# Down projection of a ConvFFN: one level of Strassen's product for the prompt, in one sweep over the weights

## The chip, the cores and the metric

The kernel runs on one core of a Trainium2 chip. Its engines are named as the profile names them: PE (matrix products; PEld is its weight load), DVE, ACT and POOL (elementwise work), and SP, which here only issues transfers (DMA). Each engine works through its own list of instructions in order. The metric is the time of one execution in microseconds.

## The reference, cut to what matters

One layer of a streaming encoder is computed for a prompt of 1024 tokens and for 8 sample streams of 16 new tokens, together 1152 tokens, in fp32. The part that is changed is the end of the layer:

```python
D_MODEL = 1024;  D_FF = 2816;  CONV_W = 3
def conv_ffn(x, prev, w_up, conv_w, conv_b, w_down):
    up = x @ w_up                                     # D_MODEL -> 2*D_FF
    up_p = jnp.concatenate([prev, up], axis=1)        # prev: zeros for the prompt
    c = sum(up_p[:, j:j + L] * conv_w[j] for j in range(CONV_W)) + conv_b
    gate, val = jnp.split(c, 2, axis=-1)
    return (jax.nn.silu(gate) * val) @ w_down, up_p[:, -(CONV_W - 1):]

f, new_conv = conv_ffn(rmsnorm(x, norm2), conv_prev, w_up, conv_w, conv_b, w_down)
x = x + f
...
y = rmsnorm(x, final_g)
```

## The kernel before, in words

Tokens stand in nine tiles of 128: eight of the prompt (`NPT`) and one with all samples. Of `w_down` (2816 x 1024) there are 22 blocks of 128 rows (`NF`, index k), each in two column halves of 512 (`dh`).

All products are of fp32 precision made from three products of rounded numbers: an operand x is split into a high part (written by ACT, type fp32r) and a low part, x minus the high part (written by DVE, by the helper `tt`, whose line in the profile is L86). `mm3` then issues three matmuls, high by high (L61), high by low (L62) and low by high (L63).

The up projection runs over 22 blocks j (gate and value columns) and already uses one level of Strassen's product: for each j `prep` makes seven weight operands `op` (sums on POOL, splits on ACT and DVE), `product` multiplies, `collect` adds the seven products into `ext`, and `up_pair_end` does the convolution, the silu and the product `g`, and stores g of block j (features by tokens) to DRAM in `g_d`. Such a block takes 22.2 us. The last store of g, j = 21, falls into the beginning of the down projection.

The down projection works in two groups of tokens, tiles 0 to 4 and then tiles 5 to 8. For each it runs over both column halves and for each of these over all k. `down_k` loads a weight tile 128x512 (`wd`, five buffers) and splits it (`wdh` by ACT on L1489, `wdl` by DVE); it also splits the activations (`gh`, L1503, and `gl`) which `reload` has brought back from `g_d` as `gr` (L1452). So each weight is loaded and split twice, 88 tiles in all, and there are 9 x 2 x 22 x 3 = 1188 matmuls of 128x512. The sums stand in PSUM, one bank for each tile (`acc`). For the last five k (`TAILK`) of the last half, the loop goes tile by tile, so that the closing normalization of one tile runs beside the matmuls of the next. The residual rows X (`x3`, 128x1024 each) and the vector `fgb` are loaded at k = 14, and `conv_out` writes the convolution state; an order is imposed there by hand:

```python
if dh == 0 and k == 14:
    with tc.issue_after(WD[COUNT[0] - 1].ins):
        ...
        load_x3()
```

Otherwise the order of instructions on each engine, SP's loads among them, is not the one in which the code is written. A scheduler of the framework (`schedule_with_timeline_sim=True`) orders each engine's list from the data dependences, the buffers and its own estimate of times. All loads and stores are issued on SP, which works them off in that order; an issue that has to wait holds up those behind it. In the listings of order, `waits DMAHW5_49` is such a wait for one of eight DMA completion counters, used in turn, and `waits DVE_49` a wait for DVE.

Of the kernel before, what the change touches and what calls it, by code (L numbers as in the profile page):

```python
# [13 lines left out]
OP = mybir.AluOpType  # L14
# [31 lines left out]
def emit(ctx, tc, x_prompt, x_sample, cache_k, cache_v, state_ssm_re, state_ssm_im, state_conv,  # L46
# [21 lines left out]
    def pool(name, bufs=1, **kw):  # L68
        return tc.tile_pool(name=name, bufs=bufs, reuse_waits="tile", **kw)
# [1216 lines left out]
    def prep(n):  # L1286

        j, i = divmod(n, 7)
        if j >= NF:
            return  # L1290
        a, b = RAW[j, 0], RAW[j, 1]
        if i == 0:
            s1 = upW.tile([P, 4, P], F32, name=f"S1_{j}", tag="S1", bufs=1)
            gsub(s1, b[:, 0], b[:, 1], OP.add)
            SUMS[j] = dict(A11=a[:, 0], A12=a[:, 1], A22=b[:, 1], S1=s1, S2=a[:, 0], S3=b[:, 0], S4=a[:, 1])
        src = SUMS[j][PROD[i][0]]
        pl = opL if i < 3 else opR
        op = pl.tile([P, 2, 4, P], F32R, name=f"op{n}", tag="op", bufs=3 if i < 3 else 4)
        act(op[:, 0], src, AF.Copy)  # L1299
# [93 lines left out]
    def up_pair_end(j):  # L1393
        cg = upw.tile([P, GLEN], F32, name=f"cg{j}", tag="cg", bufs=1)
        up_conv(j, 0, cg)
        act(cg, cg, AF.Silu)  # L1396
        g = upw.tile([P, GLEN], F32, name=f"g{j}", tag="gs")
        up_conv(j, 1, g)
        tt(g, g, cg, OP.mult)
        nc.sync.dma_start(g_d[j], g)  # L1400

    sts = ExitStack()
    stp = sts.enter_context(pool("stp", side="right"))
    up_begin(0)
# [31 lines left out]
    fu.close()  # L1436
    exs.close()
# [1 line left out]
    h2s.close()  # L1439


    gr0 = ctx.enter_context(pool("gr0"))
    dwA = ctx.enter_context(pool("dwA"))
    gr = ctx.enter_context(pool("gr", side="right"))

    HC = (slice(0, 640), slice(640, GLEN))

    def reload(half, j):
        if j < NF:
            n = HC[half].stop - HC[half].start  # L1450
            GT[half, j] = (gr0 if half == 0 and j < 4 else gr).tile([P, n], F32, name=f"gr{half}_{j}")
            nc.sync.dma_start(GT[half, j], g_d[j, :, HC[half]])  # L1452

    for j in range(4):
        reload(0, j)
    dw = ctx.enter_context(pool("dw", 2, side="right"))
    fgb = dw.tile([P, DM], F32, name="fgb", bufs=1)
    S3 = dw.tile([P, NT, 2], F32, name="S3", bufs=1)

    def conv_out():  # L1460
        cf = cvt.rearrange("p r a -> p (r a)")
        n = NROW * NF2
        outp = [(conv_prompt[0, 0].rearrange("j (a p) -> (j a) p", p=P), 0, 2 * NF2),
                (conv_sample[0].rearrange("b j (a p) -> (b j a) p", p=P), 2 * NF2, n - 2 * NF2)]
        for dst, c0, m_ in outp:
            for i in range(0, m_, P):
                m = min(P, m_ - i)
                pt = pup.tile([P, P], F32, name=f"cvo{c0}_{i}", tag="up")
                nc.tensor.transpose(pt[:m], cf[:, c0 + i:c0 + i + m], ident)  # L1469
                r = dw.tile([P, P], F32, name=f"cvr{c0}_{i}", tag="rows")  # L1470
                V_.tensor_copy(r[:m], pt[:m])
                nc.sync.dma_start(dst[i:i + m], r[:m])

    COUNT, WD = [0], {}

    def down_k(half, dh, k, nt, pl, b):
        dc = slice(dh * 512, dh * 512 + 512)
        nm = f"{half}{dh}{k}"
        w = COUNT[0]
        COUNT[0] += 1  # L1480
        main = pl is dwA

        def op_(x, n):
            return pl.tile([P, n], F32R, name=x + nm, tag=f"{x}{w % 2}" if main else x, bufs=1 if main else b)

        raw = dwA.tile([P, 512], F32, name="wd" + nm, tag=f"wd{w % WDB}")
        WD[w] = nc.sync.dma_start(raw, w_down[0, k * P:(k + 1) * P, dc])
        wh_, wl_ = op_("wdh", 512), op_("wdl", 512)
        act(wh_, raw, AF.Copy)  # L1489
        tt(wl_, raw, f(wh_), OP.subtract)  # L1490
        w5 = 5 * P if main else nt * P
        gh_, gl_ = op_("gh", w5), op_("gl", w5)

        if half == 0:
            segs = [(gh_[:, 0:640], gl_[:, 0:640], GT[0, k])]
        else:
            def smp(x):
                return x[:, 384:512].rearrange("p (b s) -> p b s", s=NS)
            g_ = GT[1, k]
            segs = [(gh_[:, 0:384], gl_[:, 0:384], g_[:, 0:384]),  # L1500
                    (smp(gh_), smp(gl_), g_[:, 384:].rearrange("p (b s) -> p b s", s=NS + 2)[:, :, 2:])]
        for oh_, ol_, src in segs:
            act(oh_, src, AF.Copy)  # L1503
            tt(ol_, src, f(oh_), OP.subtract)
        return gh_, gl_, wh_, wl_

    for half in range(2):
        t0, nt = ((0, 5), (5, 4))[half]
        X3 = {}

        def load_x3():
            for t in range(t0, t0 + nt):
                X3[t] = dw.tile([P, DM], F32, name=f"x3_{t}", tag="x3", bufs=6)
                nc.sync.dma_start(X3[t], x2_d[t * P:(t + 1) * P])

        for dh in range(2):
            dc = slice(dh * 512, dh * 512 + 512)
            last = half == 1 and dh == 1
            acc = {t: pup.tile([P, 512], F32, name=f"acc{t}{dh}", tag="up") for t in range(t0, t0 + nt)}
            ke = NF - TAILK if last else NF  # L1520
            for k in range(ke):
                if half == 0:
                    reload(dh, 4 * (1 - dh) + k)
                gh_, gl_, wh_, wl_ = down_k(half, dh, k, nt, dwA, 2)
                for t in range(t0, t0 + nt):
                    c = slice((t - t0) * P, (t - t0 + 1) * P)
                    mm3(acc[t], gh_[:, c], gl_[:, c], wh_, wl_, k == 0, k == NF - 1)
                if dh == 0 and k == 14:
                    with tc.issue_after(WD[COUNT[0] - 1].ins):
                        if half == 0:  # L1530
                            conv_out()
                            nc.sync.dma_start(fgb, bcast_row(final_g, DM))
                        load_x3()
            ops = [down_k(half, dh, k, nt, *((dwA, 2) if k < ke + 2 else (dw, TAILK - 2))) for k in range(ke, NF)]
            for t in range(t0, t0 + nt):
                for k in range(ke, NF):
                    gh_, gl_, wh_, wl_ = ops[k - ke]
                    c = slice((t - t0) * P, (t - t0 + 1) * P)
                    mm3(acc[t], gh_[:, c], gl_[:, c], wh_, wl_, k == 0, k == NF - 1)
# [44 lines left out]
```

## Time and profile before

| | |
|---|---|
| three runs | 1244.7, 1247.71, 1249.7 us; median 1247.71 |
| the profiled execution | 1247.31 us; span in the profile 1245.2 us |
| mean granted TensorE clock | 0.983 |
| busy, share of the span | PE 95%, PEld 84%, DVE 70%, ACT 52%, POOL 19% |
| moved by DMA | 149.05 MB, 120 GB/s in the mean |
| last matmul of the up projection ends | 954.6 us |
| down projection, matmuls | 956.6 to 1232.2 us |
| end of the last store | 1245.2 us |

Each row of the profile that follows names line, engine, operation, tile written and tiles read, with buffer numbers left out. Shares are means over stages with different bounds, so the rows of a single stage are what counts. "Idle before" is the time in which an engine had nothing to do before an instruction, with what ended it.

### The profile page before, as it was taken

What the parts mean: (1) busy time and instruction counts of PE and PEld (TensorE: products, weight loads), DVE (VectorE), ACT (ScalarE), POOL (GpSimd) and SP (SyncE); (2) the same over time, 40 slices, a digit from 0 to 9 for tenths busy, and PEclk for the clock granted to TensorE, in tenths of its full rate; (3) what the DMA queues carried; (4) which work ended last, traced back from release to release, by engine and by line L of the source; (5) the groups of instructions that cost most, each with busy time, mean ns of one, the idle gap of its engine ahead of it and who ended that gap; (6) DMA issues with size and microseconds to landing.
All of it is one profiled execution on the core that took longest, in us unless ns stands there. A gap on an engine that the chain in (4) does not pass through costs nothing. (4 is left out here: it accounts for less than half of the span.)

```text
span 1245.2 us, 20642 instructions
## 1 busy us (share of the span) xinstructions
PE 1186.4 (95%) x7528; PEld 1047.4 (84%) x7528; DVE 877.4 (70%) x2062; ACT 648.5 (52%) x1425; POOL 237.1 (19%) x276
## 2 busy tenths in 40 slices
PE   8999999999979878999999999999999999999995
PEld 6777776678768668999999999999998778888884
DVE  6898868898358887667676676767766446468655
ACT  7346557754366676454544545445444344355542
POOL 0000000000000112545354453544531000000000
PEclk9999999999999889999999999999999999999998
DMA  7523246649722521222222212222113982227332
GB/s 251 107 88 117 99 104 192 204 140 256 215 73 85 164 90 35 73 76 66 73 88 74 79 63 73 88 74 81 60 66 111 352 315 77 77 80 250 93 102 77
DMA packets 134023, 149.05 MB, mean 120 GB/s; under 512 B 28794, under 2 KB 94210, under 8 KB 133890
## 3 DMA queue, kind: packets, MB, share of 16 engines
q1 hardware_dynamic: 133922, 147.74, 37.3%
q8 instruction: 59, 0.97, 0.3%
q14 instruction: 42, 0.34, 0.1%
HBM read 107.06 MB, written 41.69 MB: 119 GB/s over the span
## 5 line engine op out<-in xcount | busy, mean ns | idle before, releaser
L86 DVE TENSOR_TENSOR op<-ur,op 128x512 fp32r<-128x512 f32 x132 | 117.6, 893 | 127.5 <-ACT op L1299 124.6
L62 PE MATMUL acc<-wdl,gh 128*128 128x512 f32 x396 | 154.5, 392 | 0.2 <-DVE wdl L86 0.2
L63 PE MATMUL acc<-wdh,gl 128*128 128x512 f32 x396 | 153.4, 391 | 0.0
L86 DVE TENSOR_TENSOR gl<-gr,gh 128x640 fp32r<-128x640 f32 (+2 forms) x132 | 69.7, 555 | 100.4 <-ACT gh L1503 100.0
L1299 ACT ACTIVATE op<-ur 128x512 fp32r<-128x512 f32 x132 | 83.0, 632 | 94.2 <-POOL ur L1253 41.1
L1503 ACT ACTIVATE gh<-gr 128x640 fp32r<-128x640 f32 (+2 forms) x132 | 64.1, 519 | 128.4 <-PE acc L62 121.5
L61 PE MATMUL acc<-wdh,gh 128*128 128x512 f32 x396 | 107.6, 392 | 4.0 <-ACT wdh L1489 3.1
L1253 POOL TENSOR_TENSOR S<-ur 128x512 f32<-128x512 f32 x22 | 51.7, 2352 | 232.0 <-DMA ur<-in_w_up_dram 217.1
L61 PEld LDWEIGHTS acc<-wdh,gh 128*128 128x128 f32 x396 | 74.1, 188 | 20.2 <-ACT wdh L1489 3.9
L62 PEld LDWEIGHTS acc<-wdl,gh 128*128 128x128 f32 x396 | 74.8, 189 | 16.8 <-DVE wdl L86 1.1
L63 PEld LDWEIGHTS acc<-wdh,gl 128*128 128x128 f32 x396 | 74.8, 189 | 15.5
L86 DVE TENSOR_TENSOR wdl<-wd,wdh 128x512 fp32r<-128x512 f32 x88 | 60.5, 687 | 7.8 <-ACT wdh L1489 7.6
L1489 ACT ACTIVATE wdh<-wd 128x512 fp32r<-128x512 f32 x88 | 54.3, 618 | 9.1 <-DMA wd<-in_w_down_dram 5.9
L1388 POOL COPY cvt<-ext 128x16 f32<-128x16 f32 x44 | 35.0, 796 | 94.8 <-ACT ext L1359 94.8
L1387 POOL COPY cvt<-ext 128x2 f32<-128x2 f32 x44 | 19.9, 453 | 143.9 <-DVE ext L86 143.9
L1391 DVE SCALAR_TENSOR_TENSOR cg<-ext,cw,cg 128x1168 f32<-128x1168 f32 x22 | 44.1, 2005 | 0.0
L1253 POOL TENSOR_TENSOR ur<-S,ur 128x512 f32<-128x512 f32 x22 | 38.2, 1737 | 18.2 <-DVE op L86 18.1
L61 PE MATMUL po<-oh,sh 128*128 128x512 f32 x72 | 30.1, 418 | 8.2 <-DVE xs L1213 5.7
L1253 POOL TENSOR_TENSOR ur<-ur,ur 128x512 f32<-128x512 f32 x22 | 35.8, 1627 | 1.7
L1100 POOL MEMSET L<- 128x8 f32 x4 | 0.2, 112 | 179.3 <-PE pkv L62 179.3
L63 PE MATMUL pu<-wh_u,hl 128*128 128x512 f32 x72 | 30.2, 420 | 2.8 <-DVE hl L86 2.8
L526 ACT ACTIVATE e<-sc,nm 128x192 f32<-128x192 f32 (+2 forms) x64 | 25.4, 410 | 14.0 <-DVE nm L523 10.8
(1253 smaller groups left out, 3990.2 us busy)
## 6 DMA issues: line engine op xcount, KB each, us to landing
ur<-in_w_up_dram SPq DMA_DIRECT2D x44, 512.0 KB, 3.9
wd<-in_w_down_dram SPq DMA_DIRECT2D x88, 256.0 KB, 2.9
g_d<-g SPq DMA_DIRECT2D x22, 584.0 KB, 2.9
gr<-g_d SPq DMA_DIRECT2D x22, 320.0 KB, 6.4
gr<-g_d SPq DMA_DIRECT2D x22, 264.0 KB, 5.7
wa<-a_d SPq DMA_DIRECT2D x9, 512.0 KB, 3.6
xa_d<-xo SPq DMA_DIRECT2D x9, 512.0 KB, 6.6
xs<-xa_d SPq DMA_DIRECT2D x9, 512.0 KB, 3.9
```

The costliest lines, as they stand in the source:

```text
L61: mm(out, lh, rh, start=first, stop=False, skip_group_check=True)
L62: mm(out, lh, rl, start=False, stop=False, skip_group_check=True)
L63: return mm(out, ll, rh, start=False, stop=last, skip_group_check=True)
L86: V_.tensor_tensor(o, a, b, op=op)
L526: act(e[:, r], pss[r // 2][:, r % 2], AF.Exp, bias=nm[:, r:r + 1], scale=0.125, accum_out=den[:, r:r + 1])
L1253: nc.gpsimd.tensor_tensor(o, a, b, op=op)
L1299: act(op[:, 0], src, AF.Copy)
L1387: nc.gpsimd.tensor_copy(cvt[:, 0:2, ft], ext[:, SEQ:SEQ + 2])
L1388: nc.gpsimd.tensor_copy(cvt[:, 2:, ft].rearrange("p (b j) -> p b j", j=2), es[:, :, NS:])
L1391: stt(o, ext[:, 0:GLEN], cw[:, 0, ft:ft + 1], o, op0=OP.mult, op1=OP.add)
L1489: act(wh_, raw, AF.Copy)
L1503: act(oh_, src, AF.Copy)
```

## The change

The token tiles of the prompt become two halves (tiles 0 to 3 and 4 to 7), the 22 blocks of features two halves of `NK` = 11, the columns two halves (`LO`, `HI`). So activations and weights are 2 x 2 blocks, A(h, q) and B(q, e), and the prompt's result is formed from seven products in place of eight, of which each has 11 k of four pairs of token tiles. A pair is tile p and tile p + 4.

First, in the up projection: `wd_sums` makes four sums of weight blocks (T1 to T4) and stores them in a new DRAM tensor `t_d`. There are 22 calls, one for each half of each k: two loads of 256 KB, four DVE operations of 128x256, one store of 512 KB, with a single buffer `ws`.

Second, in the down projection: one sweep over k = 0 to 10 with the four weight blocks B11, B12, B21 and B22. B11 is multiplied with the four tiles of A(0, 0) into the four banks a; all four are multiplied with the sample tile, which is not split into products, into two further banks; 24 matmuls for each k. Then come six passes of 11 k of 12 matmuls, with T1, T2, B22, T3, B21 and T4, alternately into the four banks b and the four banks a. Between passes DVE adds (`drain`) a set of banks to the halves of X while the next pass fills the other set. The activation sums `su` are made on DVE during the passes from `gr` tiles, which now stay in SBUF: 44 tiles 128x512, each loaded once. The matmuls number 11 x 24 + 66 x 12 = 1056; weight splits 110; drains 30 (28 for the prompt).

The core of the diff:

```diff
+    def wd_sums(i):
+        k, c = divmod(i, 2)
+        c = slice(c * 256, c * 256 + 256)
+        b = upw.tile([P, 4, 256], F32, name=f"ws{i}", tag="ws", bufs=1)
+        b4 = b.rearrange("p (h e) n -> p h e n", e=2)
+        for h in range(2):
+            r = (h * NK + k) * P
+            nc.sync.dma_start(b4[:, h], w_down[0, r:r + P].rearrange("p (e n) -> p e n", e=2)[:, :, c])
+        tt(b[:, 0], b[:, 1], b[:, 0], OP.subtract)
+        tt(b[:, 1], b[:, 3], b[:, 1], OP.subtract)
+        tt(b[:, 3], b[:, 3], b[:, 0], OP.subtract)
+        tt(b[:, 2], b[:, 2], b[:, 3], OP.subtract)
+        nc.sync.dma_start(t_d[k, :, :, c], b)
...
     for j in range(1, NF):
...
             if i == 2:
                 up_pair_end(j - 1)
+            if i == 4:
+                wd_sums(j)
...
-    for half in range(2):
-        t0, nt = ((0, 5), (5, 4))[half]
...
-        for dh in range(2):
...
-            for k in range(ke):
-                if half == 0:
-                    reload(dh, 4 * (1 - dh) + k)
-                gh_, gl_, wh_, wl_ = down_k(half, dh, k, nt, dwA, 2)
-                for t in range(t0, t0 + nt):
-                    c = slice((t - t0) * P, (t - t0 + 1) * P)
-                    mm3(acc[t], gh_[:, c], gl_[:, c], wh_, wl_, k == 0, k == NF - 1)
...
+    def pairs(x, k, g, w, opens, only=None):
+        for p in range(NP2) if only is None else (only,):
+            c = slice(p * P, (p + 1) * P)
+            mm3(bank(x, p, opens and k == 0), g[0][:, c], g[1][:, c], *w, opens and k == 0, k == NK - 1)
...
+    for k in range(NK):
+        w = {}
+        for blk in ("B11", "B12", "B21", "B22"):
+            w[blk] = w_op(blk, k)
+            if blk == "B11":
+                load_g(0, 0, k + 4)
+                g = g_op(GA[0, 0, k])
+                pairs("a", k, g, w[blk], True)
...
+            q, e = int(blk[1]) - 1, int(blk[2]) - 1
+            mm3(smb[e], *sm[q], *w[blk], k == 0 and q == 0, k == NK - 1 and q == 1)
+        load_gs(k + 2)
+        if k >= 4:
+            load_g(1, 0, k - 4)
+            load_g(1, 1, k - 4)
+        if k == 2:
+            conv_out()
+            nc.sync.dma_start(fgb, bcast_row(final_g, DM))
+        if k == 7:
+            load_x(NPT)
...
+    for k in range(NK):
+        w = w_op("T1", k)
+        if k < 4:
+            load_g(1, 0, k + NK - 4)
+            load_g(1, 1, k + NK - 4)
+        elif k < 8:
+            load_x(k - 4)
+        load_g(0, 1, k)
+        if k + 6 < NK:
+            sum_one(k + 6)
+        g = g_op(SU[k])
+        pairs("b", k, g, w, True)
+        tt(SU[k], SU[k], GA[0, 0, k], OP.subtract)
...
+    for p in range(NP2):
+        drain("a", p, 0, LO)
+
+    for k in range(NK):
+        w = w_op("T2", k)
+        if k < 4:
+            load_x(NP2 + k)
...
```

The order of instructions moves with it at three places.

First, SP at the end of the first sweep. `wd34` is the third weight block of k = 8, `wd36` the first of k = 9, `gr01` the tiles of A(0, 1), `x3` the residual rows. Before, around the X loads at k = 14 of the first column half:

```order
L1487 DMA wd0014_11407<-in_w_down_dram 128x512 [waits DMAHW0_49,DVE_49]
...
L1532 DMA fgb_11020<-in_final_g_dram 128x1024 [waits DMAHW3_49]
L1514 DMA x3_0_11468<-x2_d_70 128x1024 [waits DMAHW4_49]
...
L1514 DMA x3_4_11476<-x2_d_70 128x1024 [waits DMAHW0_49]
L1487 DMA wd0015_11480<-in_w_down_dram 128x512 [waits DMAHW1_49,DVE_49]
L1452 DMA gr1_16_12121<-g_d_5452 128x528 [waits DMAHW2_49]
```

and now:

```order
L1515 DMA wd34_11839<-in_w_down_dram 128x512 [waits DMAHW5_49,DVE_49]
L1481 DMA gr01_4_12169<-g_d_5452 128x512 [waits DMAHW6_49]
L1491 DMA x3_1_12196<-x2_d_70 128x1024 [waits DMAHW7_49]
...
L1481 DMA gr01_10_12327<-g_d_5452 128x512 [waits DMAHW7_49]
L1515 DMA wd35_11848<-in_w_down_dram 128x512 [waits DMAHW0_49,DVE_49]
L1491 DMA x3_4_12356<-x2_d_70 128x1024 [waits DMAHW1_49]
...
L1491 DMA x3_7_12431<-x2_d_70 128x1024 [waits DMAHW4_49]
L1515 DMA wd36_11865<-in_w_down_dram 128x512 [waits DMAHW5_49,DVE_49]
```

The loads of A(0, 1) and of X, which the code has in the passes T1 and T2, stand in SP's list ahead of the weights of k = 9 and 10 of the sweep.

Second, DVE in the up projection, block j = 3; `op25` to `op27` are low parts of weight operands of PE, `ws5` and `ws6` the new sums. Before:

```order
L86 TENSOR_TENSOR op25_6271<-ur31_6090,op25_6271 128x512 [waits DMAHW2_49,PE_49,Activation_49]
L86 TENSOR_TENSOR op26_6301<-ur31_6090,op26_6301 128x512 [waits PE_49,Activation_49]
L86 TENSOR_TENSOR ext20_6092<-pu20c_6212,ext20_6092 128x5x64 [waits PE_49]
...
L86 TENSOR_TENSOR op27_6331<-ur30_6088,op27_6331 128x512 [waits Activation_49]
L1391 SCALAR_TENSOR_TENSOR g2_6450<-ext21_6095,cw_3917,g2_6450 128x1168 [waits DVE_49]
```

and now:

```order
L86 TENSOR_TENSOR op25_6288<-ur31_6107,op25_6288 128x512 [waits DMAHW6_49,PE_49,Activation_49]
L86 TENSOR_TENSOR ws5_7053<-ws5_7053 128x256 [waits DMAHW4_49,DMAHW2_49,DVE_49]
L86 TENSOR_TENSOR ws5_7053<-ws5_7053 128x256 [waits DMAHW5_49,DVE_49]
L86 TENSOR_TENSOR ws5_7053<-ws5_7053 128x256 [waits DVE_49] x2
L86 TENSOR_TENSOR op26_6326<-ur31_6107,op26_6326 128x512 [waits PE_49,Activation_49]
...
L86 TENSOR_TENSOR op27_6356<-ur30_6105,op27_6356 128x512 [waits Activation_49]
L1389 SCALAR_TENSOR_TENSOR g2_6475<-ext21_6112,cw_3917,g2_6475 128x1168 [waits DVE_49]
L86 TENSOR_TENSOR ws6_7307<-ws6_7307 128x256 [waits DMAHW6_49,DMAHW0_49]
```

The four operations of a sum stand between operands of PE, the first of them with a wait for its two loads. The scheduler has put two sums into each of the first eleven or so blocks, where the code has one in each.

Third, DVE where the down projection begins; `g21` is the last product of g, whose store follows. Before:

```order
L1390 SCALAR_TENSOR_TENSOR g21_10985<-ext211_10765,cw_3917,g21_10985 128x1168 [waits DMAHW1_49,Activation_49]
L86 TENSOR_TENSOR wdl000_11032<-wd000_11029,wdh000_11031 128x512 [waits DMAHW7_49,Activation_49]
...
L86 TENSOR_TENSOR gl002_11090<-gr0_2_11013,gh002_11089 128x640 [waits DMAHW4_49,PE_49,Activation_49]
L86 TENSOR_TENSOR wdl002_11086<-wd002_11083,wdh002_11085 128x512 [waits DMAHW1_49,Activation_49]
L86 TENSOR_TENSOR g21_10985<-g21_10985,cg21_10978 128x1168 [waits Activation_49]
```

and now:

```order
L1388 SCALAR_TENSOR_TENSOR cg21_11155<-ext210_10931,cw_3917,cg21_11155 128x1168 [waits Activation_49]
L86 TENSOR_TENSOR sl01_11308<-gs0_1_11205,sh01_11307 128x128 [waits DMAHW3_49,Activation_49]
L86 TENSOR_TENSOR sl11_11312<-gs1_1_11207,sh11_11311 128x128 [waits DMAHW4_49,Activation_49]
L86 TENSOR_TENSOR wl0_11214<-wd0_11211,wh0_11213 128x512 [waits DMAHW5_49,Activation_49]
...
L86 TENSOR_TENSOR wl3_11273<-wd3_11270,wh3_11272 128x512 [waits DMAHW0_49,Activation_49]
L1389 SCALAR_TENSOR_TENSOR cg21_11155<-ext210_10931,cw_3917,cg21_11155 128x1168 [waits DVE_49]
...
L86 TENSOR_TENSOR g21_11162<-g21_11162,cg21_11155 128x1168 [waits Activation_49]
```

The first low weight part now stands behind three of the wide operations of the convolution instead of one, and four weight and four sample parts stand ahead of the last product of g.

More of the change, by code (lines that the diff above doesn't have):

```diff
@@ L1439, in emit @@
     h2s.close()
+    pups.close()
     gr0 = ctx.enter_context(pool("gr0"))
@@ L1444, in emit @@
     gr = ctx.enter_context(pool("gr", side="right"))
[L1446 to L1457, printed above, removed]
@@ L1458, in emit, with load_g @@
-    S3 = dw.tile([P, NT, 2], F32, name="S3", bufs=1)
+    dw = ctx.enter_context(pool("dw", side="right"))
+    pdn = ctx.enter_context(pool("pdn", space=PSUM))
+    NP2 = NPT // 2
+    WDB, TAILK = 5, 5
+    GA, GS, SU, X3 = {}, {}, {}, {}
+    def load_g(h, q, k):
+        if k < NK:
+            pl = gr0 if h == q == 0 and k < 4 else gr
+            GA[h, q, k] = pl.tile([P, 512], F32, name=f"gr{h}{q}_{k}")
+            nc.sync.dma_start(GA[h, q, k], g_d[q * NK + k, :, h * 512:h * 512 + 512])
@@ new lines, in load_gs, with load_x, operand @@
+    def load_gs(k):
+        if k < NK:
+            for q in range(2):
+                GS[q, k] = dwA.tile([P, GLEN - SEQ], F32, name=f"gs{q}_{k}", tag=f"gs{q}", bufs=3)
+                nc.sync.dma_start(GS[q, k], g_d[q * NK + k, :, SEQ:])
+    def load_x(t):
+        X3[t] = gr.tile([P, DM], F32, name=f"x3_{t}")
+        nc.sync.dma_start(X3[t], x2_d[t * P:(t + 1) * P])
+    CW, CG, SPARE = [0], [0], []
+    def operand(src, base, count, bufs, spare):
+        w = count[0]
+        count[0] += 1
+        n = src.shape[-1]
+        if spare:
+            hi, lo = (gr.tile([P, n], F32R, name=f"{base}{x}{w}", tag=SPARE.pop()) for x in "hl")
+        else:
+            hi, lo = (dwA.tile([P, n], F32R, name=f"{base}{x}{w}", tag=f"{base}{x}{w % bufs}") for x in "hl")
+        act(hi, src, AF.Copy)
+        tt(lo, src, f(hi), OP.subtract)
+        return hi, lo
@@ new lines, in w_op, with g_op @@
+    def w_op(blk, k, spare=False):
+        w = CW[0]
+        raw = dwA.tile([P, 512], F32, name=f"wd{w}", tag=f"wd{w % WDB}")
+        if blk[0] == "T":
+            src = t_d[k, :, SUM_AT[blk]]
+        else:
+            r, e = (int(blk[1]) - 1) * NK + k, int(blk[2]) - 1
+            src = w_down[0, r * P:(r + 1) * P, e * 512:e * 512 + 512]
+        nc.sync.dma_start(raw, src)
+        return operand(raw, "w", CW, 4, spare)
+    def g_op(src, spare=False):
+        return operand(src, "g", CG, 2, spare)
@@ new lines, in emit, with bank, drain @@
+    BK2 = {}
+    def bank(x, p, opens):
+        if opens:
+            BK2[x, p] = pdn.tile([P, 512], F32, name=f"dn{x}{p}_{CW[0]}", tag=f"{x}{p}")
+        return BK2[x, p]
+    def drain(x, p, h, dc):
+        o = X3[p + NP2 * h][:, dc]
+        tt(o, o, BK2[x, p], OP.add)
+    def pairs(x, k, g, w, opens, only=None):
+        for p in range(NP2) if only is None else (only,):
+            c = slice(p * P, (p + 1) * P)
+            mm3(bank(x, p, opens and k == 0), g[0][:, c], g[1][:, c], *w, opens and k == 0, k == NK - 1)
@@ new lines, in sum_one @@
+    def sum_one(k):
+        SU[k] = gr.tile([P, 512], F32, name=f"su{k}", tag=f"su{k}")
+        tt(SU[k], GA[1, 0, k], GA[1, 1, k], OP.add)
+    for k in range(NK - 5):
+        sum_one(k)
+    for k in range(NK):
[11 more added lines that the diff above has]
+        tt(SU[k], SU[k], GA[0, 0, k], OP.subtract)
+        if k == 1:
+            for e in range(2):
+                o = X3[NPT][:, (LO, HI)[e]]
+                tt(o, o, smb[e], OP.add)
+            half_one(NPT, LO)
+            half_two((NPT,), LO, HI)
@@ new lines, in emit @@
+    for p in range(NP2):
+        drain("a", p, 0, LO)
+    for k in range(NK):
+        w = w_op("T2", k)
+        if k < 4:
+            load_x(NP2 + k)
+        g = g_op(SU[k])
+        pairs("a", k, g, w, False)
+        tt(SU[k], GA[0, 1, k], SU[k], OP.subtract)
+    for p in range(NP2):
+        drain("b", p, 1, HI)
+    for k in range(NK):
+        w = w_op("B22", k)
+        g = g_op(SU[k])
+        pairs("b", k, g, w, False)
+        tt(GA[1, 0, k], GA[0, 0, k], GA[1, 0, k], OP.subtract)
+        SPARE.append(f"su{k}")
@@ new lines, in emit @@
+    for p in range(NP2):
+        drain("a", p, 0, HI)
+    for k in range(NK):
+        w = w_op("T3", k)
+        g = g_op(GA[1, 0, k])
+        pairs("a", k, g, w, False)
+    for p in range(NP2):
+        drain("b", p, 0, HI)
+        half_one(p, HI)
+    for k in range(NK):
+        w = w_op("B21", k)
+        g = g_op(GA[0, 1, k])
+        pairs("b", k, g, w, True)
+    for p in range(NP2):
+        drain("a", p, 1, HI)
+        half_one(NP2 + p, HI)
+    ops = {}
+    for k in range(NK):
+        late = k >= NK - TAILK
+        w = w_op("T4", k, k == NK - 1)
+        g = g_op(GA[1, 1, k], k >= NK - TAILK + 2)
+        if late:
+            ops[k] = g, w
+        else:
+            pairs("a", k, g, w, False)
+        if k == 2:
+            for p in range(NP2):
+                drain("b", p, 0, LO)
+            half_two(tuple(range(NP2)), HI, LO)
@@ L1556 @@
+    for p in range(NP2):
+        for k, (g, w) in ops.items():
+            pairs("a", k, g, w, False, p)
+        drain("a", p, 1, LO)
+        half_two((NP2 + p,), HI, LO)
 _INS = ['x_prompt', 'x_sample', 'cache_k', 'cache_v', 'state_ssm_re', 'state_ssm_im', 'state_conv',
```

116 lines of the change are left out of this document (49 added, 67 removed).

## The prediction

> **What bounds the kernel now.** I read four views: busy time by stretch, the PE timeline of the down projection, the groups, and the DMA rates. By stretch (start:end, length, busy us of PE, its weight loads, DVE, ACT and POOL, granted clock, DMA share, GB/s):
>
> ```profile
> 500.00:954.60 454.60, 454.60 (x3442) 454.41 (x3440) 315.14 (x424) 223.21 (x446) 213.00 (x240) 1.00 0.23 76
> 954.60:1034.00 79.40, 75.45 (x327) 61.53 (x327) 41.52 (x64) 33.04 (x54) 2.23 (x2) 0.98 0.79 283
> 1034.00:1232.20 198.20, 197.95 (x871) 162.78 (x869) 121.16 (x288) 94.25 (x209) 0.00 (x0) 1.00 0.33 105
> 1232.20:1245.20 13.00, 0.00 (x0) 0.00 (x0) 8.20 (x35) 2.89 (x5) 0.00 (x0) 0.70 0.40 161
> ...
> 955.00:960.00 5.00, 3.42 (x11) 2.77 (x12) 5.00 (x7) 3.29 (x4) 2.23 (x2) 0.74 0.47 143
> 975.00:980.00 5.00, 5.00 (x24) 4.14 (x23) 2.04 (x3) 1.91 (x3) 0.00 (x0) 1.00 1.03 406
> 975.00:1010.00 35.00, 35.00 (x157) 28.95 (x156) 14.67 (x22) 12.30 (x19) 0.00 (x0) 1.00 1.04 388
> 1005.00:1010.00 5.00, 5.00 (x25) 4.09 (x24) 2.59 (x5) 1.17 (x2) 0.00 (x0) 1.00 1.02 414
> 965.84:1011.98 46.14, 44.77 (x199) 36.46 (x197) 18.75 (x29) 16.41 (x27) 0.00 (x0) 1.00 0.99 366
> ```
>
> PE fills the up projection and the down projection (954.6 to 1232.2), at full clock after a cold start. But the first 50 us of the down projection are close to a second bound: from 975 to 1010 the DMA engines are full (share 1.04) at 388 GB/s. The PE timeline (start, length, idle before):
>
> ```profile
> 956.58 1.82 PE L61 MATMUL acc<-wdh,gh 128*128 128x512 f32 x5 [1.96 <-ACT wdh L1489]
> ...
> 959.69 0.63 PE L62 MATMUL acc<-wdl,gh 128*128 128x512 f32 x1
> 960.12 0.63 PE L63 MATMUL acc<-wdh,gl 128*128 128x512 f32 x1
> ...
> 962.06 1.30 PE L61 MATMUL acc<-wdh,gh 128*128 128x512 f32 x5
> ...
> 965.46 1.30 PE L61 MATMUL acc<-wdh,gh 128*128 128x512 f32 x5
> ...
> 1160.45 1.07 PE L61 MATMUL acc<-wdh,gh 128*128 128x512 f32 x4
> ...
> 1163.17 1.07 PE L61 MATMUL acc<-wdh,gh 128*128 128x512 f32 x4
> ...
> 1231.78 0.40 PE L63 MATMUL acc<-wdh,gl 128*128 128x512 f32 x1
> ```
>
> Fifteen matmuls from 962.06 to 965.46 are 3.40 us, twelve from 1160.45 to 1163.17 are 2.72: 0.2267 us each, whatever the tile. At 959.69 the step was 0.43: half clock.
>
> **The matmuls.** Of 1188 matmuls 1056 stay: 11 k of 24 in the first sweep (59.8 us, 5.44 each), then six passes of 11 k of 12 (179.5 us, 2.72 each). The 132 removed are 132 x 0.2267 = 29.9 us, on the path. This is all that the change can win.
>
> **The passes, and what feeds them.** Groups (count, then busy us, mean ns):
>
> ```profile
> L86 DVE TENSOR_TENSOR wdl<-wd,wdh 128x512 fp32r<-128x512 f32 x88 | 60.5, 687 | 7.8 <-ACT wdh L1489 7.6
> L1489 ACT ACTIVATE wdh<-wd 128x512 fp32r<-128x512 f32 x88 | 54.3, 618 | 9.1 <-DMA wd<-in_w_down_dram 5.9 <-PE acc L63 3.2
> L86 DVE TENSOR_TENSOR gl<-gr,gh 128x128 fp32r<-128x128 f32 x44 | 12.5, 284 | 0.0
> L86 DVE TENSOR_TENSOR x<-x,acc 128x512 f32<-128x512 f32 x18 | 11.4, 683 | 3.7 <-PE acc L63 3.7
> ```
>
> All splits and sums are 128x512 like these rows: per k of a pass DVE makes a low weight part (0.687), a low activation part (the same shape) and a sum (0.68), 2.06 of 2.72 us; ACT makes two high parts, 1.24. They hide beside PE. The 28 drains (0.683 each) stand between passes, four at a time while the next pass fills the other banks, 2.7 us; I charge 1 us in all, bounds 0 and 6 x 2.0 = 12 (four drains less the 0.66 us that DVE has free in each of the first k). In the sweep DVE has 4 low weight parts, one of 512 and two of 128 per k, 4.0 of 5.44 us. The 22 extra weight splits over before (110 for 88) lie in there.
>
> **The single DMA queue, first sweep.** This is the term that decides. SP issues in order, and the order of the changed program puts the 33 activation loads of the three quadrants that only the passes read, and all nine X tiles, ahead of the last two k of weights. In before, too, the bulk begins behind the last store of g and wd0015 stands behind it:
>
> ```profile
> 965.84 0.33 SPq L1400 DMA_DIRECT2D g_d<-g  x1
> ...
> 1003.87 0.58 SPq L1487 DMA_DIRECT2D wd<-in_w_down_dram  x1
> ...
> 1011.92 0.63 ACT L1489 ACTIVATE wdh<-wd 128x512 fp32r<-128x512 f32 x1
> ...
> 1012.61 0.73 PE L61 MATMUL acc<-wdh,gh 128*128 128x512 f32 x2 [1.18 <-ACT wdh L1489]
> ```
>
> From that store through wd0015 the program moves 16.18 MB (one store of 0.60, 34 activation loads 10.22, five X 2.62, eight weights 2.10, the rest 0.64); the weight was split at 1011.92, so 46.1 us, and PE waited 1.18 us for it. In the changed program the store through wd36 (the first weight of k=9) carries 24.19 MB: the store, 28 weights 7.34, 40 activation loads 10.49, twelve sample loads 0.88, nine X 4.72, the rest 0.76. The first 16.18 MB at 46.1 us, the other 8.0 at 0.40 MB/us (between the 388 and 414 GB/s above) 19.8 us, together 65.9.
>
> The last store itself is later. Ahead of the last product of g DVE had three 640-wide and three 512-wide low parts; now two 512-wide and four 128-wide low parts of activations, four of weights, and four 128-wide copies: 6 x 0.687 + 8 x 0.284 = 6.4 us against 3 x 0.824 + 3 x 0.687 = 4.5 (0.824 from the row below), so +1.8, and the store goes at 967.6.
>
> ```profile
> L86 DVE TENSOR_TENSOR gl<-gr,gh 128x640 fp32r<-128x640 f32 x43 | 35.4, 824 | 67.8 <-ACT gh L1503 67.7
> ```
>
> So wd36 is in at 967.6 + 65.9 = 1033.5 and split at 1034.1. If only PE counted, k=9 would begin at 956.6 + 9 x 5.44 = 1005.6, plus some 5 for the cold clock and the later low parts: 1010.9. PE stands about 23 us in waits in k=6 to k=9. This eats most of the 29.9. After the wait: k=9 and 10, 10.9 us, and a cold start, priced by the one above: nine steps, 9 x (0.43 - 0.2267) = 1.8, taken as 1.9 with the wait for its first low part. The sweep ends at 1046.9. Bounds of the stall: 24.19 MB at 414 GB/s is 58.4 us, 7.5 less; at the 366 of the last row quoted in the first fence, 66.1, the same within 0.2. A third bound, that the small sample loads cost more than their bytes, adds at most twelve times the 0.65 us that one 0.26 MB load takes at 0.40, 7.8.
>
> The Trainium skill, "DMA: Bandwidth & Descriptors" (Where 436 GB/s comes from), lets the HBM side, some 358 GB/s for a core, bind transfers between HBM and SBUF. By it the 8.0 MB would take 22.4 us, 2.6 more, and the time would be 1246.6; the trace disagrees, since 388 stood for 35 us, and I go by the row.
>
> **The sums of weights, up projection.** 22 sums, two in each of the first eleven periods of 22.2 us. DVE is in order there; one period:
>
> ```profile
> 700.79 1.30 DVE L86 TENSOR_TENSOR op<-ur,op 128x512 fp32r<-128x512 f32 x1 [1.84 <-ACT op L1299]
> ...
> 710.06 0.69 DVE L86 TENSOR_TENSOR op<-ur,op 128x512 fp32r<-128x512 f32 x1 [4.26 <-ACT op L1299]
> ...
> 722.99 1.30 DVE L86 TENSOR_TENSOR op<-ur,op 128x512 fp32r<-128x512 f32 x1 [1.84 <-ACT op L1299]
> ```
>
> DVE is idle 1.84 + 4.26 = 6.1 us of 22.2. A sum is four operations 128x256: between 0.284 (128 wide) and 0.687 (512 wide), by line 0.42, so 1.7 a sum and 3.4 a period; if each cost 0.55, 4.4. Both fit in 6.1. Its DMA, 1 MB a sum, is 2.1 MB a period or 94 GB/s beside the 76 of the first row: far from 388. I charge 1.5 us for disturbances, bounds 0 and the second rival's.
>
> **The end and the sum.** The last tile's normalization stays 13.0 us (fourth row). Sweep end 1046.9, passes 179.5, drains 1, sums 1.5, tail 13.0: span 1241.9. The profiled run took 1247.31 with a span of 1245.2, 2.1 outside: 1244.0. The median of the runs, 1247.71, lies 0.4 above. That is -3.3 us, -0.27%. About 0.5%, 1241.1 to 1253.5, is what a measurement can tell from no change.
>
> The Trainium skill, "TensorE: Matmul & The Clock Gate" (Part 1: The HAM clock gate), has the clock fall to half after a window of some 3.4 us without work and need as long of work to return, which loses 1.7 us each time. The stall above may come in several pieces, since wd35 and wd36 stand apart; by this rule each further piece of that length would add 1.7, so 1245.7 with two pieces. I count one.
>
> **Rivals.**
> First: the transfers are hidden, or rearranged by the hardware, and PE alone sets the sweep. For it: before, at 99% DMA share, PE waited only 1.18 us. Against: 8.0 MB more are ahead of the same weights. Without the 23 us and the cold start: 1244.0 - 23 - 1.9 = about 1219, 2.2% faster. Chance 0.10.
> Second, slower: the sums hold DVE up. Buffer ws is single: loads wait until the store of the sum before is done, and the first operation of a sum stands in DVE's order ahead of PE's operands. If it waits w, a period costs 2 x (1.7 + w); beyond 6.1, at w over 1.35 us, PE is held. At w = 2 it is 1.3 a period, 14 us in eleven, 1258; at w = 3, 3.3 a period, 36 us, 1280. For it, by the DMA rows (KB each, us to landing):
>
> ```profile
> wd<-in_w_down_dram SPq DMA_DIRECT2D x88, 256.0 KB, 2.9
> g_d<-g SPq DMA_DIRECT2D x22, 584.0 KB, 2.9
> ```
>
> A store and then a load take 5.8 us, against the eleven between sums. Chance 0.12.
> Third: passes bound by hand-over between ACT, DVE and PE, since a pass has two buffers of activations only. 0.1 to 0.2 us a k in 66 k, 6 to 12 us: 1250 to 1256. DVE's 2.06 of 2.72 speaks against. Chance 0.06.
>
> **The numbers.** Forecast case 0.72, its own range 1236 (the stall's 7.5 less) to 1252 (the 7.8 more). Of it about 0.22 lies under 1241.1, 0.50 within. With the first rival faster is 0.32; with half of the third (0.03) same is 0.53; the second and the rest of the third 0.15 slower. For 8 in 10 the range takes the forecast and the near part of both sides: 1230 to 1256; the first rival (0.10) and most of the second (0.10) stay outside.
>
> **What would show it.** In the changed kernel: a stretch after 975 with the DMA full for some 55 us and PE idle some 20 us, waiting for ACT's high weight parts and those for the DMA; the nine X tiles landing in it; then 66 k of 2.72 us with the DMA near 96 GB/s (0.262 MB in 2.72 us). Up periods of 22.2 us with ws operations in DVE's gaps. Wrong if PE's wait in the sweep is under 10 us, if periods of the up projection grow, or if a k of a pass is over 2.85 us.

## The result, and the profile after

The changed kernel takes 1277.05 us (median of four runs, 1275.93 to 1278.92). Beside runs of the kernel before, the ratio is 1.0239, interval 1.0209 to 1.0269: 2.4% slower. The forecast was 1244.0 in a range of 1230 to 1256. The profiled execution has a span of 1277.1 us, 31.9 more than before.

The changed kernel by stretches; the columns are as in the prediction:

```profile
500.00:987.40 487.40, 463.48 (x3457) 458.34 (x3456) 355.12 (x510) 220.34 (x451) 207.72 (x243) 1.00 0.35 113
...
1083.60:1263.70 180.10, 180.08 (x793) 148.34 (x791) 126.15 (x238) 94.07 (x168) 0.00 (x0) 1.00 0.36 104
...
1263.70:1277.10 13.40, 0.00 (x0) 0.00 (x0) 8.78 (x38) 2.89 (x5) 0.00 (x0) 0.61 0.39 157
...
987.40:1083.60 96.20, 76.94 (x273) 57.67 (x272) 66.63 (x121) 43.41 (x83) 0.86 (x2) 0.82 0.91 319
```

The first row is the rest of the up projection: its last matmul ends at 987.4 instead of 954.6, 32.8 us later. Of these 1.8 lie ahead of it (its first matmul, into `pu00a`, begins at 447.3 instead of 445.5), where the change does nothing; the up projection itself is 31.0 longer. PE was idle for 23.9 of 487.4 us where before it was never idle. The first sweep (the last row here) lasts 96.2 us, with a mean clock of 0.82. The six passes take 180.1 us and PE has no gap in them. So against the forecast span of 1241.9 the up projection is 31.3 us later than charged (32.8 less 1.5), the sweep is 3.9 longer (96.2 against 1046.9 - 954.6 = 92.3), the passes are 0.4 shorter (180.1 against 180.5), the tail is 0.4 longer: 35.2 in all (1277.1 less 1241.9).

The stretch 510 to 720, in which the sums are made, in the kernel before and then in the changed kernel:

```profile
510.00:720.00 210.00, 210.00 (x1594) 210.00 (x1593) 151.80 (x202) 105.28 (x208) 104.53 (x115) 1.00 0.24 77
```

```profile
510.00:720.00 210.00, 189.69 (x1398) 185.76 (x1397) 155.72 (x237) 88.28 (x182) 81.32 (x98) 0.99 0.47 149
```

The waits of the changed kernel there, of SP, of DVE and of POOL for the up weights (us in total, times, longest):

```profile
SPq L1417 <- DVE ws L86: 75.5, 16, 8.6
SPq L1417 <- DMA ws<-in_w_down_dram: 48.2, 20, 3.8
SPq L1412 <- DMA t_d<-ws: 34.7, 17, 2.8
```

```profile
DVE ws L86 <- DMA ws<-in_w_down_dram: 53.7, 26, 5.3
...
POOL S L1253 <- DMA ur<-in_w_up_dram: 6.2, 7, 1.0
```

DVE is busy 155.72 us and waits 53.7 for the loads of the sums: 209.4 of 210. Nothing of its idle time is left, and PE falls from 210.00 busy to 189.69. What PE waits for is put down to ACT's operations on `ext`; ACT in turn waits 43.8 us for POOL (17.6 before), and POOL 98.1 us for DVE (63.2 before). SP has 158 us of waits that all belong to the sums, but the up weights come in time: POOL waits 6.2 us for them (1.1 before). Part of a block, on DVE's timeline and on SP's:

```profile
585.18 0.41 DVE L86 TENSOR_TENSOR ws<-ws 128x256 f32<-128x256 f32 x1
...
588.20 0.68 DVE L86 TENSOR_TENSOR op<-ur,op 128x512 fp32r<-128x512 f32 x1
592.05 0.42 DVE L86 TENSOR_TENSOR ws<-ws 128x256 f32<-128x256 f32 x1 [3.17 <-DMA ws<-in_w_down_dram]
592.91 1.35 DVE L86 TENSOR_TENSOR ws<-ws 128x256 f32<-128x256 f32 x3 [0.43 <-DMA ws<-in_w_down_dram]
594.18 0.68 DVE L86 TENSOR_TENSOR op<-ur,op 128x512 fp32r<-128x512 f32 x1
...
585.62 0.56 SPq L1417 DMA_DIRECT2D t_d<-ws  x1
588.87 1.20 SPq L1412 DMA_DIRECT2D ws<-in_w_down_dram  x2
```

The last operation of one sum is at 585.18, its store at 585.62, the next loads, which need the buffer, at 588.87. DVE has nothing else to do from 588.88, 3.3 us after the sum before, and waits. The operand at 594.18 stands behind a sum that had to wait 3.6 us (3.17 and 0.43) for its two loads. The block around these rows, from one product of g on DVE (560.42) to the next (585.51), takes 25.1 us instead of 22.2.

The sweep of the changed kernel, on SP, ACT and PE (from the timelines) and as rows by stretch:

```profile
1000.75 0.33 SPq L1398 DMA_DIRECT2D g_d<-g  x1
...
1063.47 0.63 ACT L1503 ACTIVATE wh<-wd 128x512 fp32r<-128x512 f32 x1 [6.46 <-DMA wd<-in_w_down_dram]
...
1069.28 2.62 ACT L1503 ACTIVATE wh<-wd 128x512 fp32r<-128x512 f32 x4 [3.26 <-DMA wd<-in_w_down_dram]
...
1069.96 2.07 PE L61 MATMUL dna<-wh,gh 128*128 128x512 f32 x4 [3.86 <-ACT wh L1503]
```

```profile
1040.00:1070.00 30.00, 16.56 (x46) 10.66 (x44) 14.14 (x26) 6.63 (x14) 0.00 (x0) 0.73 1.04 394
1010.00:1060.00 50.00, 42.47 (x156) 31.46 (x154) 36.87 (x66) 22.05 (x44) 0.00 (x0) 0.90 1.03 371
```

The DMA engines are full (share 1.03 and 1.04) at 371 to 394 GB/s, and the first weight of k = 9 is split at 1069.28, 68.5 us after the last store of g began; 65.9 to landing had been forecast.

### The profile page after: what moved, and what is told of

Its sections match the earlier page's. It is cut to its first block, busy times and chain, and to the rows that moved or that the text cites. A ratio compares the mean times of both kernels' runs of the same rounds, so it can differ in the third digit from the quotient of the medians.

```text
span 1277.1 us, 20721 instructions
## 1 busy us (share of the span) xinstructions
PE 1183.2 (93%) x7396; PEld 1036.6 (81%) x7396; DVE 947.6 (74%) x2159; ACT 654.1 (51%) x1414; POOL 227.1 (18%) x276
## 5 line engine op out<-in xcount | busy, mean ns | idle before, releaser
L1503 ACT ACTIVATE wh<-wd 128x512 fp32r<-128x512 f32 x110 | 68.8, 630 | 39.8 <-DMA wd<-in_w_down_dram 19.5
L86 DVE TENSOR_TENSOR wl<-wd,wh 128x512 fp32r<-128x512 f32 x110 | 74.7, 686 | 16.5 <-ACT wh L1503 16.2
L86 DVE TENSOR_TENSOR ws<-ws 128x256 f32<-128x256 f32 x88 | 40.8, 463 | 61.7 <-DMA ws<-in_w_down_dram 60.9
L62 PE MATMUL dna<-wl,gh 128*128 128x512 f32 x176 | 71.7, 407 | 0.7 <-DVE wl L86 0.7
L61 PE MATMUL dna<-wh,gh 128*128 128x512 f32 x176 | 67.3, 415 | 3.9 <-ACT wh L1503 3.9
L63 PE MATMUL dna<-wh,gl 128*128 128x512 f32 x176 | 56.8, 405 | 0.0
L62 PE MATMUL dnb<-wl,gh 128*128 128x512 f32 x132 | 51.4, 389 | 0.0
L61 PE MATMUL dnb<-wh,gh 128*128 128x512 f32 x132 | 51.0, 390 | 0.0
L1503 ACT ACTIVATE gh<-gr 128x512 fp32r<-128x512 f32 x44 | 27.5, 628 | 35.2 <-PE dna L62 22.3
L61 PEld LDWEIGHTS dna<-wh,gh 128*128 128x128 f32 x176 | 34.7, 200 | 12.3 <-ACT wh L1503 5.3
L62 PEld LDWEIGHTS dna<-wl,gh 128*128 128x128 f32 x176 | 35.0, 199 | 9.0 <-DVE wl L86 1.4
L63 PEld LDWEIGHTS dna<-wh,gl 128*128 128x128 f32 x176 | 34.9, 198 | 7.7
```

The costliest lines, as they stand in the source:

```text
L61: mm(out, lh, rh, start=first, stop=False, skip_group_check=True)
L62: mm(out, lh, rl, start=False, stop=False, skip_group_check=True)
L63: return mm(out, ll, rh, start=False, stop=last, skip_group_check=True)
L86: V_.tensor_tensor(o, a, b, op=op)
L1503: act(hi, src, AF.Copy)
```

## The experiments

Each is an edit of the changed kernel, where nothing else is said. Times are medians, ratios are against runs of the kernel before on the same chip (1246.4 to 1247.1 us; 1247.7 for the changed kernel, so a difference between two medians is good to a microsecond or so).

### The sums alone, added to the kernel before

```diff
             if i == 2:
                 up_pair_end(j - 1)
+            if i == 4:
+                wd_sums(j)
```

> The kernel before with the sums of weights added to its up projection (loads, four DVE operations, store of t_d), and its own down projection left as it was; nothing reads t_d. Theory A (the sums cost 33 us because DVE waits in order for their loads): 1248 + 31 to 35 = 1279 to 1283, with DVE idle some 60 us for ws loads and the up projection as long as in the changed kernel. Rival B (the sums hide, and the 33 us come from the new order of the rest of the program): 1247 to 1252.

1277.78 us, ratio 1.025 (1.0222 to 1.0278), just under the range of theory A. DVE waits 60.8 us for the loads of the sums, as in the changed kernel (60.9 over all 22). The up projection part of the change is the whole loss against before, and the down projection as it was ordered gained nothing.

### One sum in each block

```diff
             if i == 4:
-                wd_sums(j)
+                with tc.issue_after(UPD[-1].ins):   # UPD: the loads of the up weights
+                    wd_sums(j)
```

> The changed kernel with each sum's loads tied behind the load of the up weights of its own block, so that there is one sum in each of 22 blocks and not two in each of the first eleven; DVE's work, bytes and the single buffer are the same. Theory A (a period is held only when two sums and their two waits exceed the 6.1 us that DVE has free): one sum with a wait of 2.8 is 4.5 us, hidden; 1277 - 28 to 33 = 1244 to 1249. Rival B (a wait costs its length wherever it stands, since PE's operands stand behind it): no change within 5 us, 1272 to 1282.

1246.33 us, ratio 0.9993 (0.9977 to 1.0008): 30.7 us less than the changed kernel, with the same work and bytes. The same stretch, and DVE's waits in it:

```profile
510.00:720.00 210.00, 210.00 (x1594) 210.00 (x1593) 173.14 (x238) 105.42 (x208) 98.56 (x115) 1.00 0.39 124
```

```profile
DVE op L86 <- ACT op L1297: 26.4, 9, 3.2
DVE ws L86 <- DMA ws<-in_w_down_dram: 9.8, 10, 2.2
```

PE is never idle again, and DVE has 26.4 us left in which it waits for ACT's operands, the kind of idle time that it had before (59.2). One sum in a block is hidden, and so are its waits, which speaks against rival B. The waits are shorter here too: 21.7 us over all 22 sums, 1.0 each instead of 2.8. This run alone does not tell the spacing from the shorter waits.

### No sums, transfers only, operations only

Three kernels tell apart what in the sums costs the time. In all three the passes read raw blocks of `w_down`, so the prompt's result is not computed.

```diff
-            src = t_d[k, :, SUM_AT[blk]]
+            r, e = k, SUM_AT[blk] % 2
+            src = w_down[0, r * P:(r + 1) * P, e * 512:e * 512 + 512]
```

> The changed kernel without the sums of weights: the passes T1 to T4 read raw blocks of w_down in place of t_d (so the prompt's result is not computed), all other work as in the changed kernel. It prices the whole of the sums: theory A 1277 - 31 to 35 = 1242 to 1246; a rival (the sums' price lies partly in the down projection, through t_d's own loads): over 1250.

1245.79 us, ratio 0.9998 (0.9984 to 1.0011). The sums cost 1277.05 - 1245.79 = 31.3 us.

```diff
     def wd_sums(i):
...
-        tt(b[:, 0], b[:, 1], b[:, 0], OP.subtract)
-        tt(b[:, 1], b[:, 3], b[:, 1], OP.subtract)
-        tt(b[:, 3], b[:, 3], b[:, 0], OP.subtract)
-        tt(b[:, 2], b[:, 2], b[:, 3], OP.subtract)
```

> As no_sums, but with the 44 loads and 22 stores of the sums and without their 88 DVE operations (raw blocks are stored to t_d and not read). Theory A (DVE's wait in order is the cost, not the bytes): within 4 us of no_sums, 1242 to 1249. Rival C (the added 22 MB slow the loads of the up weights): most of the 33 us, 1265 to 1278.

1271.34 us, ratio 1.0203 (1.0177 to 1.0229): 25.6 us over the kernel without sums, and DVE has no part in it. Theory A, that transfers without DVE's wait cost nothing, fails. The stretch, and what SP and POOL wait for:

```profile
510.00:720.00 210.00, 190.74 (x1390) 189.42 (x1389) 123.83 (x176) 90.67 (x182) 77.92 (x99) 0.95 0.48 155
```

```profile
SPq L1413 <- DMA ws<-in_w_down_dram: 48.2, 19, 4.0
SPq L1412 <- DMA t_d<-ws: 46.0, 17, 3.3
```

```profile
POOL S L1253 <- DMA ur<-in_w_up_dram: 50.1, 5, 13.0
```

Now POOL, which makes the first sums of the up weights, waits 50.1 us for their loads (6.2 in the changed kernel, 1.1 before). SP itself stood 94 of 210 us before stores that need a load in flight, and before loads that need the one buffer back from a store. The loads of the up weights are queued behind. But the order is not that of the changed kernel: without the operations there are three or four sums in a block, not two (stores to `t_d` between two stores of g on SP's timeline). Their loads go out every 7.8 us (504.86, 512.62, 520.56), so three or four keep SP for 23 to 31 us, more than the 22.2 of a block; two would be some 16, by an estimate from the same times. This is a second way in which the sums can cost time, and not that of the changed kernel, where the up weights came in time.

```diff
+        if i == 0:
+            ...                                    # load one block, once
-        nc.sync.dma_start(t_d[k, :, :, c], b)
...
+            if j < 12 and i in (1, 4):
+                with tc.issue_after(OPI[-1].ins):  # OPI: DVE's low parts of operands
+                    wd_sums(2 * j - 2 + i // 4)
```

> As no_sums, but with the 88 DVE operations on one block that stays in SBUF, loaded once and not stored, eight operations in each of the first eleven blocks, tied on DVE behind operands of the same block. Theory A (3.4 us of work in 6.1 us of idle time costs nothing without waits): 1243 to 1250. Rival D (DVE's idle time is not usable, since ACT and DVE take turns on the operands): 3.4 x 11 = 37 us, 1275 to 1285; half of it, 1262.

1245.73 us, ratio 0.9995 (0.998 to 1.0009), no cost at all. In the stretch DVE is busy 188.30 us and PE 210.00:

```profile
510.00:720.00 210.00, 210.00 (x1594) 210.00 (x1593) 188.30 (x274) 105.34 (x209) 112.93 (x114) 1.00 0.24 77
```

So the work of the sums hides, as the prediction had it. What does not hide is the work together with its waits.

### Two buffers

```diff
-        b = upw.tile([P, 4, 256], F32, name=f"ws{i}", tag="ws", bufs=1)
+        b = upw.tile([P, 4, 256], F32, name=f"ws{i}", tag="ws", bufs=2)
-        g = upw.tile([P, GLEN], F32, name=f"g{j}", tag="gs")
+        g = upw.tile([P, GLEN], F32, name=f"g{j}", tag="gs", bufs=1)
```

> The changed kernel with two buffers for the sums, and one for g in place of two to make room. The order then has three sums in a block, seven blocks long. Theory A (it is the sum of work and waits in a block against 6.1 us that counts): three sums are 5.1 us of work; with waits of 0.5 to 2 each 0.5 to 5 us a block over, 4 to 35 us in all against 33, so 1248 to 1279. Rival E (the single buffer is the whole cause): 1242 to 1248.

1271.85 us, ratio 1.0218 (1.0196 to 1.024). The single buffer alone is not the cause. With two, DVE waits less for the loads, 24.2 us over all sums instead of 60.9, 1.1 a sum. But the scheduler puts three or four sums into a block, and all 22 run in some six blocks (473.9 to 638.2): 22 x (1.7 + 1.1) - 6 x 6.1 = 25 us, for 26.1 measured against the kernel without sums. So theory A holds, at fewer blocks than it had. The single buffer of g, which this kernel shares with the next two, costs nothing there.

### The same transfers taken apart, then the same sums taken apart

In both, a sum is taken apart: its loads are issued one sum ahead of its operations and its store, tied behind the load of the up weights. There are two in each of eleven blocks, as in the changed kernel.

```diff
+    def wd_sums(i):
+        with tc.issue_after(UPD[-1].ins):
+            if i < NF:
+                ...                                # two loads into one of two buffers
+        if i > 0:
+            b = WS[i - 1]
+            with tc.issue_after(OPI[-1].ins):
+                tt(b[:, 0], b[:, 1], b[:, 0], OP.subtract)
+                ...
+            with tc.issue_after(LD[-1].ins):       # LD: the loads of the sums
+                nc.sync.dma_start(t_d[k, :, :, c], b)
```

Without the DVE operations, the passes reading raw blocks:

> As traffic_only (loads and stores of the sums, no DVE operations, raw blocks in the passes), again two in each of eleven blocks and the same bytes, but with two buffers and one for g, and the store of a block put behind the loads of the next, all behind the load of the up weights, so that SP seldom waits for a transfer under way. Theory F (in traffic_only SP's own in-order waits, for ws loads and for t_d stores, kept the loads of the up weights back): 1243 to 1251, POOL's waits for ur under 10 us. Rival C (the bytes themselves slow the up projection): 1265 to 1272.

1247.25 us, ratio 0.9998 (0.9984 to 1.0012), and the stretch carries more traffic than any other; below it, what SP still waits for:

```profile
510.00:720.00 210.00, 210.00 (x1595) 210.00 (x1594) 152.25 (x202) 105.35 (x209) 102.87 (x114) 1.00 0.53 172
```

```profile
SPq L1416 <- DMA t_d<-ws: 45.1, 10, 5.9
```

POOL waits 2.9 us for the up weights instead of 50.1, although SP still waits 45.1 us for stores to give a buffer back. The bytes cost nothing. What cost time in the transfers-only kernel was how they stood in SP's order, three or four sums in a block and ahead of the up weights; the two were not tried apart.

With all operations, the passes as in the changed kernel:

> The changed kernel with all of its sums, two in each of eleven blocks, but taken apart in the same way: two buffers (one for g), the loads of a sum issued one sum ahead of its DVE operations and its store. Work, bytes and density as in the changed kernel, without most waits. Theory G (only waits cost, on DVE for the loads and on SP for loads, DVE and stores): 1244 to 1252. Rival H (two sums in a block are too much work beside the rest, with or without waits): 1262 to 1277.

1247.12 us, ratio 0.9988 (0.9972 to 1.0003): 29.9 us less than the changed kernel at the same density of work. The stretch, and the waits of SP and POOL:

```profile
510.00:720.00 210.00, 210.00 (x1593) 209.97 (x1592) 165.75 (x275) 104.04 (x209) 95.95 (x112) 1.00 0.54 169
```

```profile
SPq L1416 <- DMA t_d<-ws: 60.9, 18, 4.8
...
POOL S L1253 <- DMA ur<-in_w_up_dram: 31.2, 9, 4.3
```

DVE no longer waits for a load of a sum, and PE is busy 210.00 of 210. Rival H is out: two sums in a block are not too much work. Of theory G the part on DVE holds. SP's waits are only in part gone: it stands longer before stores' buffers than in the changed kernel (60.9 us for 34.7), and POOL waits longer for the up weights (31.2 for 6.2), and this costs nothing here.

### The order of loads in the sweep

`LASTW` is the list of weight loads in the order of the code.

```diff
+            with tc.issue_after(LASTW[-1].ins):
                 load_g(1, 0, k - 4)
                 load_g(1, 1, k - 4)
...                                                # the same at load_x and in T1, T2
```

> The changed kernel with the loads of A(1,0), A(1,1), A(0,1) and of X tied in SP's order behind the weight load beside which the code has them. Theory A (the bulk loads ahead of the weights hold the sweep up by some 18 us and a cold start): 1277 - 18 to 22 = 1255 to 1259, PE's waits in the sweep under 4 us. Rival B (the DMA engines are the bound of the sweep whatever the order): 1272 to 1277, waits for wh move to the passes.

1250.33 us, ratio 1.0033 (1.0016 to 1.0049): 26.7 less than the changed kernel, more than the 18 to 22 expected. PE waits in the sweep 2.4 us for weights (0.7 + 1.5 + 0.2), and 1.6 more at the beginning of the first pass, instead of 16.2 (9.4 + 3.9 + 2.2 + 0.7). The stretch from the last up matmul to the first pass is:

```profile
982.90:1053.80 70.90, 65.19 (x274) 50.96 (x273) 59.06 (x109) 41.56 (x82) 0.86 (x2) 0.98 0.94 312
```

The first pass begins at 1052.98, so the sweep takes 70.1 us instead of 96.2, 26.1 less; what follows it is 2.0 longer. By the two rows some 13.6 of the gain is idle time of PE (19.3 and 5.7), and 11.8 is busy time: 76.94 us for 273 matmuls at a clock of 0.82, and 65.19 for 274 at 0.98. The loss in the sweep was therefore idle time and, by more than a single cold start, a low clock.

```diff
         elif k < 8:
+            with tc.issue_after(LASTW[-1].ins):
-            load_x(k - 4)
+                load_x(k - 4)
...                                                # the same at load_x in T2
```

> The changed kernel with only the eight prompt X loads tied behind the weights beside which the code has them; the activation loads stay early. 4.2 MB less ahead of the first weight of k = 9: at 0.40 MB/us 10.5 us. Theory A (bytes ahead of the weights set the sweep's end): 1277 - 9 to 12 = 1265 to 1268. Rival (X is the whole cause, since only these stand directly ahead of the last weights): 1250 to 1255.

1263.41 us, ratio 1.0119 (1.0103 to 1.0136): 13.6 less, where 9 to 12 were expected. 4.2 MB of 24.2 give half of what all reordering gives, so X is not the whole cause, and the bytes ahead of the weights set the end. The sweep itself, from the last up matmul (981.7) to the first pass (1066.8), takes 85.1 us in the profile, 11.1 less than 96.2, for 10.5 forecast. The rest of the difference lies ahead of the sweep, where this edit does nothing: the first matmul into `pu00a` begins at 442.3 in this profile and at 447.3 in that of the changed kernel.

### Both edits

The edits of "One sum in each block" and of "The order of loads in the sweep" together.

> Both edits together. If the two losses are independent: 1277 - 33 - 20 = 1224 (1220 to 1230), faster than the kernel before by about 2%. Rival (they share a cause, or the passes become the bound once the sweep is fed): 1235 to 1250.

1221.69 us, ratio 0.98 (0.978 to 0.9821): 2.0% faster than the kernel before. The gains are 30.7 and 26.7, and 55.4 together: nearly independent. Its up projection (the row ends 1.7 us ahead of before's last up matmul), its sweep, and the passes up to 1205:

```profile
500.00:952.90 452.90, 452.90 (x3429) 452.73 (x3427) 364.07 (x505) 224.33 (x446) 199.04 (x237) 1.00 0.38 123
...
952.90:1023.80 70.90, 66.22 (x273) 52.86 (x272) 57.55 (x107) 42.04 (x81) 0.86 (x2) 0.93 0.93 304
1023.80:1205.00 181.20, 178.81 (x781) 147.21 (x780) 130.90 (x242) 92.87 (x166) 0.00 (x0) 0.99 0.47 154
```

It gains 25.2 us of the 29.9 that the 132 fewer matmuls are worth. The first matmul of the sweep begins 4.0 us after the end of the up projection, 956.93 after 952.93, where before it was 2.0 (956.58 after 954.6), and in the first pass PE waits 2.4 us for a low weight part (181.20 less 178.81); the rest of the difference was not followed further.

## Why the prediction was wrong

**The step that failed** is the sums of weights, the term of 1.5 us. It counted DVE's work (3.4 of 6.1 us of idle time in a block), which is right: the operations measured 0.425 us in the median, for 0.42, and without waits they cost nothing (operations only, 1245.73). For all else it charged 1.5 us, and that measured 31.0 in the profiles and 31.3 against the kernel without sums. What the sum put at nothing, and left to a rival, is that DVE stands still before the first operation of a sum until its loads are in. The second rival had the place, the price and the point from which it decides: waits over 1.35 us a sum. DVE waited 60.9 us in 22 sums, 2.8 each, for which that rival's formula gives 2 x (1.7 + 2.8) - 6.1 = 2.9 a block, 32 in eleven, and the block measured 25.1 for 22.2. It had been given a chance of 0.12, and its 1280 stood outside the range. The argument against it was that a store and a load, 5.8 us by the rows, fit into the eleven between sums. That compares means. In the changed kernel DVE came to a sum 3.3 us after the end of the one before (588.88 after 585.59), since the work between them was not spread evenly: SP issues the loads only once the store has come back, and DVE is at its operation before they land. The listing of order had the first operation of `ws6` only a little behind those of `ws5`.

That the waits on DVE are the cause is shown by three runs together: the sums alone, added to the kernel before, cost 31 us with 60.8 us of such waits; the operations without waits cost nothing; and the whole sums, two in a block, cost nothing once DVE found its loads there, although SP still waited 60.9 us for stores in the stretch. The transfers-only kernel shows a second price, on SP, at three or four sums in a block: 25.6 us. At the two of the changed kernel its trace does not show it (POOL waits 6.2 us for the up weights). What SP's waits alone would cost at two in a block was not tried; by the estimate of 16 us in 22.2 they would fit.

**The matmuls and the passes** were right: 180.1 us without a gap for 179.5 and 1. So the third rival, 6 to 12 us in the passes, did not come either.

**The DMA queue in the sweep** was right in kind and near in size: 92.3 us forecast, 96.2 measured, with the DMA full at 371 to 394 GB/s. In the Trainium skill, "DMA: Bandwidth & Descriptors" (Where 436 GB/s comes from), some 358 GB/s would bind there; the 394 from 1040 to 1070 and the 371 over 50 us disagree, as the rows before did. The loads came 2.6 us later (68.5 for 65.9 and the split; 8.0 MB at 0.40 MB/us are 20.0 us, not the 19.8 in that sum). The price of the stall was slightly under-sized: 23 us and 1.9 were charged, the reordered kernel gave 26.7 back. The wait came in several pieces, and the cold clock with it: between 1040 and 1075 many matmuls stood 0.43 us apart, at a granted clock of 0.50 (0.73 in the mean of the row from 1040), where the prediction counted one restart. There the sum was still right, since the transfers and not PE set the end of the sweep (with 4.2 MB less ahead it took 11.1 us less); only the gain from reordering it was underestimated. The rule that the prediction quotes from the Trainium skill, "TensorE: Matmul & The Clock Gate" (Part 1: The HAM clock gate), pointed that way, with more loss for each further piece of some 3.4 us. The trace agrees in part: a clock of 0.50 follows the waits of 5.88 and 3.86 us (matmuls at 1064.15 and 1069.96), but it also stands from 1051.2 to 1055.0, where the longest wait in the nine us before is 1.62 us.

**The first rival** (transfers hidden) was wrong: in the sweep they were not.

**The tail** took 13.4 us, for 13.0.

## What to carry to other kernels

An engine's idle time hides added work only as far as the work and its waits fit into it together. An instruction in an in-order queue that waits for a transfer costs its work and its wait, and holds all behind it. So the price of an added step is (work plus wait) per period against the idle time of that period, asked for each queue it stands in, that of the transfers too. A load, its use and its store written as one unit on a single buffer made such waits here; issuing the loads one unit ahead, or spacing the units, took the loss away at the same work and bytes. Where a scheduler may move loads forward, bytes that are needed later can go ahead of bytes that are needed now; count what stands ahead of the next needed load, and tie the later ones behind it.

## What the runs showed of the hardware that was not expected

Transfers of 23 MB more over the up projection (177.89 MB in all, 154.82 without sums), at 172 GB/s and a DMA share of 0.53 in the stretch, cost nothing that the runs can tell (1247.25 us and 1245.79, ratio 0.9998 in both), where they were issued behind the up weights. And a sweep that is starved in pieces lost clock as well as time: 0.82 in the mean over 96.2 us, against 0.98 when fed in order.
